# A copy by DMA alone: eight rows per engine walked to and fro

## The chip, the cores and the metric

The kernel runs on one core of one Trainium2 chip. The metric is the time of one execution in microseconds (us), measured on the device. Beside it there is one execution recorded by the hardware profiler; "the profile" and "the trace" are what it left.

## The reference

```python
def setup_inputs():
    return {
        "x": np.random.randn(8192, 8192).astype(np.float32),
    }

def reference(x: np.ndarray) -> np.ndarray:
    return np.fft.ifftshift(x)
```

On an array of even sizes this swaps opposite quadrants: out[i, j] = x[(i + 4096) % 8192, (j + 4096) % 8192]. Nothing is computed; 268.4 MB are read and 268.4 MB are written, all in the chip's main memory (HBM). A row is 8192 x 4 bytes = 32 KB.

## The kernel before, in words

The kernel is a row of DMAs from the input tensor to the output tensor, memory to memory; no tile is kept on the core and no compute engine works. All DMAs are issued by SyncE (SP) through the helper `copy` (lines 25 to 29, where line 26 is the line that the profile shows). It takes a row and a column of the output, adds half of the rows and half of the columns (modulo the size) for the input, and uses the same list of steps and counts (`dims`) on both sides.

The loop (lines 35 to 39) goes down the output in stripes of 128 rows (`rows` = 16 engines x `apart` = 8), 64 stripes in all. In each stripe it issues four DMAs, one for each quarter of the columns (`piece` = 2048 floats, 8 KB): the first quarter (column 0), the third (4096), the second (2048), the fourth (6144). Each DMA is 128 rows of 8 KB, 1 MB; it is spread over 16 DMA engines, so that an engine has eight pieces of 8 KB per DMA. The kernel is written for an engine to have eight neighbouring rows, 32 KB from one to the next and 256 KB from one engine's first row to the next engine's. Each engine goes down its eight rows in one quarter, jumps back to its first row for the next quarter, and after four quarters goes on to the next stripe.

What sets the order: SP issues the 256 DMAs in the order of the program. The framework gives them eight semaphores in turn, so that from the ninth on, a DMA is issued only when the one eight before it has landed. No DMA depends on the data of another.

Of the kernel before, what the change touches and what calls it, by code (L numbers as in the profile page):

```python
# [1 line left out]

# [4 lines left out]


ENGINES = 16  # L10


@with_exitstack
def kernel(
    ctx: ExitStack,
    tc: tile.TileContext,
    x: bass.AP,
    out: bass.AP,
):
    nc = tc.nc  # L20
    R, C = x.shape
    hr = R // 2
    hc = C // 2

    def copy(queue, row, col, dims):
        queue.dma_start(
            out=bass.AP(out.tensor, out.offset + row * C + col, dims),
            in_=bass.AP(x.tensor, x.offset + (row + hr) % R * C + (col + hc) % C, dims),
        )


    apart = 8
    piece = hc // 2
    rows = ENGINES * apart
    for row in range(0, R, rows):
        for col in (0, hc):
            copy(nc.sync, row, col, [[C, rows], [1, piece]])
        for col in (piece, hc + piece):
            copy(nc.sync, row, col, [[C, rows], [1, piece]])


# [1 line left out]
_INS = ['x']  # L43
_OUTS = [((8192, 8192), 'float32')]


def kernel(**inputs):
    import numpy as _np
    import concourse.bacc as _bacc
    import concourse.tile as _tile  # L50
    from concourse import mybir as _mybir
    from concourse.bass_utils import run_bass_kernel_spmd as _run

    nc = _bacc.Bacc("TRN2", target_bir_lowering=False, num_devices=1)  # L54
    arrays, args = {}, []
    for name in _INS:
        a = _np.ascontiguousarray(inputs[name])
        if a.dtype.kind in "iu":
            a = a.astype(_np.int64)
        arrays[f"in_{name}_dram"] = a  # L60
        args.append(nc.dram_tensor(f"in_{name}_dram", a.shape, _mybir.dt.from_np(a.dtype), kind="ExternalInput").ap())
    for i, (shape, dtype) in enumerate(_OUTS):
        dt = _mybir.dt.from_np(_np.dtype(dtype))
        args.append(nc.dram_tensor(f"out_{i}_dram", shape, dt, kind="ExternalOutput").ap())
    with _tile.TileContext(nc) as tc:
        kernel(tc, *args)
    r = _run(nc, [arrays], core_ids=[0])
    got = tuple(r.results[0][f"out_{i}_dram"] for i in range(len(_OUTS)))
    return got[0]
```

## Time and profile before

| what | value |
|---|---|
| median of 3 runs | 814.22 us (814.01, 814.22, 817.59) |
| the profiled execution's own time | 813.0 us |
| its span, first to last instruction | 811.2 us |
| DMAs | 256, of 1 MB each |
| packets of their queue (q1) | 36,864; 98.8% of 16 engines' span |
| median from issue to landing of a DMA | 25.2 us |
| one issue on SP, median | 511 ns |
| read and written together | 662 GB/s over the span |

How to read it: a packet is one contiguous run moved by one DMA engine, here 8 KB of a row, and for each engine and DMA a tiny one that reports the end to a semaphore. The share of a queue is the time that its packets took, summed, by 16 engines' span. The GB/s of the page count each byte once, as it is moved; the memory sees it twice, read and written. "Issue to landing" runs from the instruction on SP to the moment when the last of 16 engines has reported. A line of the windows gives the window, its length, the busy time of GpSimd (which has four small fills at the start and no part in the copy), the clock of TensorE (unused here), the mean busy share of the DMA engines, and GB/s. A line of the waits names who waited, for what, how long in total, how many times, and the longest wait in us.

### The profile page before, as it was taken

What the parts mean: (1) busy time and instruction counts of PE and PEld (TensorE: products, weight loads), DVE (VectorE), ACT (ScalarE), POOL (GpSimd) and SP (SyncE); (2) the same over time, 40 slices, a digit from 0 to 9 for tenths busy, and PEclk for the clock granted to TensorE, in tenths of its full rate; (3) what the DMA queues carried; (4) which work ended last, traced back from release to release, by engine and by line L of the source; (5) the groups of instructions that cost most, each with busy time, mean ns of one, the idle gap of its engine ahead of it and who ended that gap; (6) DMA issues with size and microseconds to landing.
All of it is one profiled execution on the core that took longest, in us unless ns stands there. A gap on an engine that the chain in (4) does not pass through costs nothing. (4 is left out here: it accounts for less than half of the span.)

```text
span 811.2 us, 301 instructions
## 1 busy us (share of the span) xinstructions
POOL 0.2 (0%) x4
## 2 busy tenths in 40 slices
POOL 0000000000000000000000000000000000000000
DMA  8999999999999999999999999999999999999998
GB/s 303 336 329 330 334 336 332 331 333 332 333 333 336 335 335 330 336 331 332 332 332 336 329 336 330 336 327 330 334 336 325 334 334 330 332 330 330 338 330 299
DMA packets 36866, 268.47 MB, mean 331 GB/s; under 512 B 4096, under 2 KB 4096, under 8 KB 4096
## 3 DMA queue, kind: packets, MB, share of 16 engines
q1 hardware_dynamic: 36864, 268.45, 98.8%
q14 instruction: 2, 0.02, 0.0%
HBM read 268.44 MB, written 268.44 MB: 662 GB/s over the span
## 5 line engine op out<-in xcount | busy, mean ns | idle before, releaser
L54 POOL MEMSET const-bfloat16-1.0<- 128x1 bf16 x1 | 0.1, 101 | 0.0
L54 POOL MEMSET const-uint8-127<- 128x1 uint8 x1 | 0.1, 101 | 0.0
L54 POOL MEMSET const-float32-0.0<- 128x1 f32 x1 | 0.1, 98 | 0.2 <-issue 0.2
L54 POOL MEMSET const-float32-1.0<- 128x1 f32 x1 | 0.1, 98 | 0.0
## 6 DMA issues: line engine op xcount, KB each, us to landing
out_dram<-in_x_dram SPq DMA_DIRECT2D x256, 1024.0 KB, 25.2
```

Of the source, the lines that this page charges most:

```text
L54: nc = _bacc.Bacc("TRN2", target_bir_lowering=False, num_devices=1)
```

## The change

The DMAs, their sizes and the order of the quarters stay. The helper now writes a DMA as three steps: 16 engines, each 8 rows (256 KB) from the next; 8 rows per engine; 2048 columns. For the first and second quarter (the first and third DMA of a stripe) the eight rows are taken downward as before; for the third and fourth quarter (the second and fourth DMA) they are taken upward: the start is the engine's last row, and the step from row to row is minus 32 KB, on both the input and the output side. So an engine goes down in the first quarter, up in the third, down in the second, up in the fourth. In the compiled program the downward DMAs are merged again to 128 x 2048, and the upward ones stand as 16 x 8 x 2048. The order of the instructions on SP and the waits are otherwise the same.

```diff
-    def copy(queue, row, col, dims):
+    def copy(queue, row, col, per, size, down):
+
+        first = row if down else row + per - 1
+        dims = [[per * C, ENGINES], [C if down else -C, per], [1, size]]
         queue.dma_start(
-            out=bass.AP(out.tensor, out.offset + row * C + col, dims),
-            in_=bass.AP(x.tensor, x.offset + (row + hr) % R * C + (col + hc) % C, dims),
+            out=bass.AP(out.tensor, out.offset + first * C + col, dims),
+            in_=bass.AP(x.tensor, x.offset + (first + hr) % R * C + (col + hc) % C, dims),
         )
 
 
-    apart = 8
+    per = 8
     piece = hc // 2
-    rows = ENGINES * apart
-    for row in range(0, R, rows):
-        for col in (0, hc):
-            copy(nc.sync, row, col, [[C, rows], [1, piece]])
-        for col in (piece, hc + piece):
-            copy(nc.sync, row, col, [[C, rows], [1, piece]])
+    for row in range(0, R, ENGINES * per):
+        for k, col in enumerate((0, hc, piece, hc + piece)):
+            copy(nc.sync, row, col, per, piece, k % 2 == 0)
```

## The prediction

> **What bounds the kernel now.** I read the page first, then the DMA queue's own waits, then the windows, then the single packets.
>
> The page shows no compute at all; the DMA engines carry the span from the second slice to the last:
>
> ```profile
> span 811.2 us, 301 instructions
> ...
> DMA  8999999999999999999999999999999999999998
> GB/s 303 336 329 330 334 336 332 331 333 332 333 333 336 335 335 330 336 331 332 332 332 336 329 336 330 336 327 330 334 336 325 334 334 330 332 330 330 338 330 299
> DMA packets 36866, 268.47 MB, mean 331 GB/s; under 512 B 4096, under 2 KB 4096, under 8 KB 4096
> ...
> q1 hardware_dynamic: 36864, 268.45, 98.8%
> ...
> HBM read 268.44 MB, written 268.44 MB: 662 GB/s over the span
> ...
> out_dram<-in_x_dram SPq DMA_DIRECT2D x256, 1024.0 KB, 25.2
> ```
>
> See here: 256 DMAs of 1 MB; 36,864 packets, of which 4,096 (16 for each DMA) are tiny and the other 32,768 are the 8 KB pieces of rows; the 16 engines are busy 98.8% of the span; and the rate is flat at about 332 GB/s.
>
> Is it the issuing queue that holds them back? The waits of SP, and the instructions of line 26:
>
> ```profile
> SPq L26 <- DMA out_dram<-in_x_dram: 649.3, 248, 3.3
> ```
> ```profile
> L26 SPq DMA_DIRECT2D out_dram<-in_x_dram x256: 511/511/666, 0.7 to 785.8; - x128
> ```
>
> No. An issue takes 511 ns, 256 of them 131 us; SP waits 649.3 / 248 = 2.62 us ahead of each of the last 248 issues for a DMA that is eight back. The page's 25.2 us to landing is eight DMAs at one per 3.15 us (811.2 less about 4 us of start and end, by 256).
>
> So each DMA engine always has packets; what matters is how long one takes. The windows of the start against the middle:
>
> ```profile
> 2.00:5.00 3.00, 0.00 (x0) 1.00 0.89 328
> 5.00:8.00 3.00, 0.00 (x0) 1.00 1.00 350
> 8.00:11.00 3.00, 0.00 (x0) 1.00 1.01 352
> 11.00:14.00 3.00, 0.00 (x0) 1.00 1.00 341
> 100.00:400.00 300.00, 0.00 (x0) 1.00 0.99 333
> 400.00:700.00 300.00, 0.00 (x0) 1.00 0.99 332
> ```
>
> The last number is GB/s: the same engines with the same share of busy time move 350 to 352 for 6 us, and 332 ever after. The trace's packet records say more. Of the 32,768 packets of 8 KB, 60.0% take 309 ns (309 to 312), the other 40.0% take 511.7 ns on average; the mean is 390.2 ns. Check: 32,768 x 390.2 / 16 = 799.0 us, and 4,096 tiny ones of 9 ns add 2.3 us: 801.3 us, the page's 98.8%. If every packet took 309 ns the data would need 633 us. So an engine's own speed is not the limit: **the memory, read and written at once, stalls four packets in ten.** Only a change in how often it stalls moves the time.
>
> **The change, part by part.** The sum starts from the profiled execution's own 813.0 us: 811.2 of span and 1.8 around it. It lies 1.2 us under the median of the runs, 814.22, and I add those 1.2 at the end.
>
> 1. *What stays.* 256 DMAs, each 16 engines by 8 rows by 8 KB; the same order of quarters (first, third, second, fourth); the same waits on the DMA eight back. The same packets in number and size: 0 us.
>
> 2. *The upward DMAs as instructions.* Compiled, the 128 downward ones are still 128 rows of 2,048; the 128 upward ones become 16 by 8 by 2,048. The trace has no issue of that shape. Below: no cheaper than 511 ns would help, since SP waits anyway. Above: the cover is the 2.62 us wait, and the longest issue in the trace is 666 ns; even at five times 511 ns the wait absorbs it (3.15 us is the interval). If that cover were gone, each upward DMA would delay the next by what it takes over 3.15 us. I take 0.
>
> 3. *The order of the rows in the upward DMAs.* A step from one row to the next is 32 KB back instead of 32 KB forward. The trace has no backward step within a DMA, but each DMA's start is a jump: back by seven rows and sideways (192 times per engine, three in each of the 64 stripes of 128 rows), or on by 121 rows to the next stripe (63 times). If I sort the 8 KB packets by start and cut them into 128s, one cut to a DMA (engines run up to 2 us apart, so the cut is rough), the first 16 packets of a cut average 397 ns after a jump back and 396 ns after a jump to a new stripe. Two very different jumps cost the same, so a sign should cost little: 0, with the bounds of step 4.
>
> 4. *The turns.* At the 192 turns inside stripes, an engine's last row is now its next row too, 16 KB to the side (or, between the third and second quarter, 8 KB), both in x and in out. Before, it moved seven rows away. The trace has no such neighbour step, so I bound it by the two classes of packets. Best: the packet behind a turn is always of the 309 class: (390.2 - 309) x 192 = -15.6 us. Worst: always of the slow class: (511.7 - 390.2) x 192 = +23.3 us. A weaker guide lies between: by the same cuts, the four quarters of a DMA average 404, 392, 380 and 384 ns. The first two rows are 14 ns over the mean of 390, the most that seems to hang on a DMA's beginning: 2 rows x 14 ns x 192 = 5.4 us, which a smoother turn could win and a rougher one pay again. The nearest row is the 397 against 396 above: no dependence on the jump. I take 0.
>
> 5. *Engines close together.* At a turn an engine that leads is back on the row number that a laggard is still on, in another block of eight rows (256 KB apart); before, it was on row 0 while the other was on row 7. Does sharing a row number cost? From the landing records, the spread (standard deviation) of the 16 engines' ends of a DMA grows from 281 ns in the first 32 DMAs to 445 ns between the 193rd and 224th, while the windows stay at 333 and 332 GB/s. Sorted by spread in four equal groups, DMAs follow at 3,151, 3,139, 3,169 and 3,148 ns, with no direction. So 0.
>
> Sum: 813.0 + 0 = 813.0, plus 1.2: **814 us, no change.**
>
> The Trainium skill has a rule that speaks against the change: "DMA: Bandwidth & Descriptors", section "Latency and other measured facts", reports copies whose parallel streams lie a large power of two apart falling from 214 to 164 GB/s at 2 MiB, and to 207 at 512 KiB, and supposes that lock-stepped streams meet on the same channels. Here the engines are 256 KiB apart in both kernels, and the trace's first 2 us, where they are closest in step, have nearly all packets at 309 ns: it does not bear the rule out at this distance. By that rule the turns would push the time towards the slower rival below.
>
> **The rivals.**
>
> *Faster: the memory still has the row at hand.* If an adjacent piece of a row just touched is cheaper, the packets behind 192 turns gain. Place: the first packet of the third, second and fourth quarter. For it: stalls come from the memory, and 350 GB/s in the window from 5 to 11 us proves that it can go faster. Against it: only 3 of 32 packets per engine and stripe are affected, and the 397 and 396 above. Fully it gives 814.2 - 15.6 = 799 us, at half the effect 806. Were the rate of the first windows held throughout (351 instead of 332.5), 268.4 MB would take 765 instead of 807 us: 772 is the floor that I don't expect.
>
> *Slower: the neighbour collides.* The packet behind a turn reads and writes beside what its own predecessor is still doing (in the records a packet starts some 3 ns ahead of the end of the one before), or beside another engine on the same row number. Fully slow: 814.2 + 23.3 = 837.5; at half, 826. It decides from 21 ns per turn on (4.1 us by 192). For it: a packet's cost is two-valued, and the slow class is well populated; with the rows taken backwards, any look-ahead in the memory would be lost on half of the DMAs too. Against it: step 5.
>
> *The change does not do what it says.* The downward DMAs carry no 16 by 8 shape. If their 128 rows are dealt to the engines in another way than eight neighbours each, no engine meets its own row at a turn, and the time stays at 814.
>
> **How the numbers follow.** No change 0.37 (814); faster 0.26; slower 0.31; not doing what it says 0.06 (814). About 0.5%, 4.1 us, is what a measurement of this kernel can tell from no change, so 810 to 818 is "the same". Of the faster case nearly all lies under 810, of the slower one nearly all over 818: faster 0.26, same 0.43, slower 0.31. The range reaches from near the full price of the faster rival to midway between half and full price of the slower: 801 to 832.
>
> **What would show it.** In the page after: still 36,864 packets on q1 and about 98.8%; GB/s between 325 and 338 in each slice. SP: about 2.6 us of wait per issue; an issue of the upward form under 3 us. Packets: the share of 309 ns still near 60%. Steps 3 and 4 are wrong if that share, or the mean of the first 16 packets of a cut (397), moves by over 20 ns against the rest of the DMA; the slower rival shows there as slow packets at the beginning of the cuts, the faster as 309s. Step 5 is wrong if the pace falls where the spread of the landings is small. What would make the whole wrong: a stall share that moves everywhere and not just at the turns, since then the order of the rows sets the pace as a whole.

## The result, and the profile after

The changed kernel takes 812.83 us (median of 22 runs, 811.92 to 813.99), the kernel before 814.37 us (22 runs, 811.77 to 819.77): ratio 0.9977, 95% interval 0.9967 to 0.9988. The forecast was 814, no change, with 810 to 818 counted as the same. The lowest runs are equal, 811.77 and 811.92; the gain lies in the bulk, since the middle half of the runs before is 813.8 to 815.2 and after 812.4 to 813.4.

The page of the changed kernel, the lines that answer to those of before:

```profile
span 810.6 us, 301 instructions
...
GB/s 303 331 334 330 336 334 330 336 333 327 335 335 332 329 332 332 337 334 331 334 331 336 326 331 337 332 334 335 330 332 334 336 332 328 333 333 336 337 330 301
DMA packets 36866, 268.47 MB, mean 331 GB/s; under 512 B 4096, under 2 KB 4096, under 8 KB 4096
...
q1 hardware_dynamic: 36864, 268.45, 99.3%
...
HBM read 268.44 MB, written 268.44 MB: 662 GB/s over the span
...
out_dram<-in_x_dram SPq DMA_DIRECT2D x256, 1024.0 KB, 25.2
```

The same packets at the same 662 GB/s, the same 25.2 us to landing. The span is 0.6 us shorter. Its waits of SP, and the instructions of line 29 (smallest, median, largest duration in ns):

```profile
SPq L29 <- DMA out_dram<-in_x_dram: 633.7, 248, 3.2
```
```profile
L29 SPq DMA_DIRECT2D out_dram<-in_x_dram x256: 537/603/700, 0.7 to 784.7; - x128
```

Issues have become longer: in turn 537 and 603 ns, 572 on average instead of 515. The waits have become shorter by about as much: 633.7 / 248 = 2.56 us instead of 2.62. The cover took it. The windows (last number GB/s):

```profile
2.00:5.00 3.00, 0.00 (x0) 1.00 1.00 330
5.00:8.00 3.00, 0.00 (x0) 1.00 1.00 355
8.00:11.00 3.00, 0.00 (x0) 1.00 1.02 344
11.00:14.00 3.00, 0.00 (x0) 1.00 1.02 339
100.00:400.00 300.00, 0.00 (x0) 1.00 1.00 333
400.00:700.00 300.00, 0.00 (x0) 1.00 1.00 333
```

Again a fast start and then 333 without end. In the packet records 60.2% of the 8 KB packets are of the 309 ns class (60.0% before) and the others average 517.2 ns (511.7). The mean of all is 391.9 ns, where it was 390.2: packets are a little longer in the kernel that is a little faster, and the engines are busy for 99.3 instead of 98.8% of the span.

One thing in these records looked like a mechanism. Cut into 128s as in the prediction, the packets of downward DMAs average 384 ns and those of upward ones 400 ns, and at the turn to the third quarter the first 16 packets average 383 ns, where they had 403 before. (At the turn to the second quarter they rose from 391 to 410, and at the turn to the fourth they went from 397 to 391; the three turns together went from 397 to 395.) So three theories went to the chip: **A**, meeting its own row at a turn saves an engine about 10 ns; **B**, the upward form as such saves; **C**, upward is dear and the turns pay for it; against them the prediction's own, that the order of an engine's rows sets nothing.

### The profile page after: what moved, and what is told of

It reads as the page before. It is cut to its first block, busy times and chain, and to the rows that moved or that the text cites. A ratio compares the mean times of both kernels' runs of the same rounds, so it can differ in the third digit from the quotient of the medians.

```text
span 810.6 us, 301 instructions
## 1 busy us (share of the span) xinstructions
POOL 0.2 (0%) x4
## 3 DMA queue, kind: packets, MB, share of 16 engines
q1 hardware_dynamic: 36864, 268.45, 99.3%
## 6 DMA issues: line engine op xcount, KB each, us to landing
out_dram<-in_x_dram SPq DMA_DIRECT2D x256, 1024.0 KB, 25.2
```

## The experiments

They ran in three sets, each with the kernel before on the same chip: all upward, turning with few meetings, two rows straight and two rows turning on chip 15; the two repeats, two rows with few meetings and the pairs by row on chip 13; the rest on chip 6. On these chips the kernel before takes 823.4 to 823.9 us, 1.1% more than in the result, so only ratios are compared, and ratios of different sets are ratios from different chips.

**All upward, no turn.**

```diff
-        for k, col in enumerate((0, hc, piece, hc + piece)):
-            copy(nc.sync, row, col, per, piece, k % 2 == 0)
+        for col in (0, hc, piece, hc + piece):
+            copy(nc.sync, row, col, per, piece, False)
```

> All 256 DMAs take their eight rows upward (16 x 8 x 2048), so there is no turn: each DMA begins seven rows below the end of the one before. Beside before at 814.4 us and the changed kernel at 812.8 (ratio 0.9977). Theory A, the turns gain: with the turns gone the gain is gone, ratio 1.000 (0.999 to 1.001). Theory B, it is the upward form (direction, or 16 x 8 instead of 128 rows) that gains, wherever the rows lie: twice as many upward DMAs, ratio 0.995. Theory C, two effects cancel: in the trace of the changed kernel the packets of downward DMAs average 384 ns and those of upward ones 400 ns, so upward is dear and the turns pay for it: all upward costs up to (400 - 390) ns x 2,048 packets per engine = 20 us, ratio 1.01 to 1.025.

Measured: 824.21 us, ratio 1.0002 (0.9990 to 1.0014). B and C both fall: 256 upward DMAs of the 16 x 8 x 2048 form cost what 256 downward ones of 128 x 2048 cost. Their issues on SP:

```profile
L29 SPq DMA_DIRECT2D out_dram<-in_x_dram x256: 571/571/690, 0.7 to 796.5; - x128
```

So the 384 against 400 ns of the cut packets was no pace. The landing records (the mean of the 16 engines' ends of a DMA, from the tenth DMA on; a mean here is good to about 10 ns) say so too: in the changed kernel a DMA of the first quarter (down) ends 3,180 ns behind the one ahead of it, of the third (up) 3,099, of the second (down) 3,156 and of the fourth (up) 3,167; before, all down, it was 3,164, 3,126, 3,140 and 3,177. The upward DMAs of the changed kernel come 35 ns sooner than its downward ones, although their packets average 16 ns longer. And in the next kernel, which also goes down and up in turn, the downward packets average 403 ns and the upward ones 389: the sign is turned round.

**Turning with few meetings.** The directions alternate as in the change, but between two stripes. The expectation counts no meeting; one in eight steps is still one, since the fourth quarter of stripe two (up) is followed by the first quarter of the same stripe (down). That makes 32 meetings per engine instead of 192, 24 KB to the side in the output and 8 KB in the input.

```diff
-    for row in range(0, R, ENGINES * per):
-        for k, col in enumerate((0, hc, piece, hc + piece)):
-            copy(nc.sync, row, col, per, piece, k % 2 == 0)
+    stripe = ENGINES * per
+    for row in range(0, R, 2 * stripe):
+        one, two = row, row + stripe
+        for k, col in enumerate((0, hc, piece, hc + piece)):
+            copy(nc.sync, (one, two)[k % 2], col, per, piece, k % 2 == 0)
+        for k, col in enumerate((0, hc, piece, hc + piece)):
+            copy(nc.sync, (two, one)[k % 2], col, per, piece, k % 2 == 0)
```

> Half of the DMAs go downward and half upward, in turn as in the changed kernel, but neighbours in time work on two different stripes of 128 rows, so no engine meets the row that it has just left. Theory A (the turns gain): ratio 1.000, as before. Theory B (the upward form gains): 0.9977, as the changed kernel. Theory C (upward is dear, turns pay): no turn to pay, so slower, up to (400 - 390) ns x 1,024 = 10 us, ratio 1.005 to 1.012. If alternation itself matters because it keeps the engines in step (spread of landings 230 to 312 ns in the changed kernel, 281 to 445 before): 0.9977 with the small spread.

Measured: 822.67 us, 0.9984 (0.9972 to 0.9996), so C falls here too; A is not yet told from "alternation alone". Both kernels then went side by side on chip 13, the changed one and this one:

> The changed kernel once more, on the same chip as the three others of this call. If its gain is real and of its size, the ratio to before is 0.9977 again (0.9967 to 0.9988), whatever the chip's own level. Theory A' (alternating directions gains, the meeting at the turn does nothing): the same ratio as no_meeting_again within 0.001. Theory A (the meeting gains): below it by 0.0015 or more.

> The kernel of no_meeting unchanged, beside the changed kernel itself; the first time it came out at 0.9984 (0.9972 to 0.9996), between the two theories. Alternation alone gains (A'): 0.9977 to 0.9984. The meeting at the turn gains (A): 1.000.

Measured: the changed kernel 822.36 us, 0.9994 (0.9980 to 1.0007); with few meetings 822.85 us, 0.9997 (0.9986 to 1.0007). They differ by 0.0003, far inside either interval: at eight rows 160 meetings more or less do nothing that can be measured, and the 0.0023 of the first comparison comes back as 0.0006, with an interval that holds 1. Nor does alternation keep the engines in step, as one line of the first expectation supposed: the spread of a DMA's 16 ends, by groups of 32 DMAs, is 230 to 311 ns in the first trace of the changed kernel, but 250 to 439 in its trace on chip 13, and was 280 to 445 before.

**More meetings per packet.** One DMA takes two quarters row by row, so that half of all packets follow their neighbour in the same row.

```diff
...
+        def dims(across):
+            return [[per * C, ENGINES], [C, per], [across, 2], [1, size]]
-            out=bass.AP(out.tensor, out.offset + first * C + col, dims),
-            in_=bass.AP(x.tensor, x.offset + (first + hr) % R * C + (col + hc) % C, dims),
+            out=bass.AP(out.tensor, out.offset + row * C + col, dims(hc)),
+            in_=bass.AP(x.tensor, x.offset + (row + hr) % R * C + hc + col, dims(-hc)),
...
-        for k, col in enumerate((0, hc, piece, hc + piece)):
-            copy(nc.sync, row, col, per, piece, k % 2 == 0)
+        for col in (0, piece):
+            copy(nc.sync, row, col, per, piece)
```

> One 2 MB DMA takes two quarters of eight rows per engine, row by row: first the one quarter of a row, then the other quarter of the same row 16 KB to the side, then the next row. So 1,024 of an engine's 2,048 packets follow their neighbour, where the changed kernel has 192 such turns. If meeting one's own row gains 10 ns: ratio 0.987. If it costs 7 ns: 1.009. If it is worth nothing: 0.998 to 1.001 (1,024 steps at nothing; 128 DMAs instead of 256 save 2,048 tiny packets of 9 ns over 16 engines, 1.2 us). At the full prices of the prediction's two classes of packets: 0.90 or 1.15.

Measured: 821.94 us, 0.9988 (0.9976 to 0.9999), that is -1.0 us with about 1.0 us to either side. The expectation puts the 2,048 tiny packets saved at 1.2 us; whether they count at all is doubtful, as the two-row kernels below show. If they don't, 1,024 neighbour steps gain 1 ns each, with 1 ns to either side; if they do, nothing. Theory A is dead at its 10 ns, and so are the full prices of both rivals. The page of this run shows fewer packets, and the mean rate that the changed kernel has on this chip too, 327 GB/s:

```profile
DMA packets 34817, 268.45 MB, mean 327 GB/s; under 512 B 2048, under 2 KB 2048, under 8 KB 2048
```

**More turns per row.** Two rows per engine and DMA (1,024 DMAs of 256 KB): straight, turning, and turning with few meetings (as above, with stripes of 32 rows, so 128 meetings instead of 768). All three have the first edit, the straight kernel the second too.

```diff
-    per = 8
+    per = 2
...
-            copy(nc.sync, row, col, per, piece, k % 2 == 0)
+            copy(nc.sync, row, col, per, piece, True)
```

> Stripes of 32 rows: an engine has two rows of a quarter per DMA, all downward; 1,024 DMAs of 256 KB. It is the control of two_rows_turning. All theories: at or above the time before, since there are four times as many DMAs (12,288 more tiny packets, at 9 ns and 16 engines 7 us, if nothing hides them) and the engines' blocks are 64 KB instead of 256 KB apart; 815 to 835 us. 1,024 issues of 511 ns are 523 us and stay covered.

> As two_rows_straight, but to and fro: 256 stripes with three turns each, 768 turns per engine instead of 192. Theory A (each turn saves (814.4 - 812.5) us / 192 = about 10 ns): 7 to 8 us under two_rows_straight. Theory B (upward form, half of the DMAs as in the changed kernel): 1.5 to 2 us under it. Theory C: of both signs, but a difference of several us. No effect of order at all: equal within 1 us.

> Two rows per engine and DMA, downward and upward in turn as in two_rows_turning, with the same mix of instruction forms, but neighbours in time lie in two different stripes of 32 rows, so no row is met at a turn. two_rows_straight had 0.9988 and two_rows_turning 1.0051. If the meeting at 768 turns is what cost 0.6 per cent there (the prediction's slower rival, 5.1 us / 768 = 7 ns per turn): 0.999. If it is the longer issue of the mixed forms (603 against 510 ns in those traces, at an interval of only 0.8 us per DMA): 1.005. If alternation as such gains, as A' has it: 0.997.

Measured: straight 823.06 us, 0.9988 (0.9975 to 1.0001); **turning 828.17 us, 1.0051 (1.0034 to 1.0068)**, on the same chip; turning with few meetings 822.89 us, 0.9994 (0.9983 to 1.0006), on chip 13. Here is the only case in which to and fro lengthens the time by more than the noise.

The straight kernel says something of the bound as well. It has 12,288 more tiny packets than the kernel before, 7 us by the expectation if nothing hid them, and it takes no longer. Its 8 KB packets average 393.9 ns, where they average 398.9 in the all-upward kernel on the same chip: 5 ns less on 2,048 packets of an engine is 10 us, so the large packets give back what the tiny ones take, as they would if something behind the engines set the pace.

The loss of the turning kernel isn't the longer issue. SP's waits, first the turning kernel, then the one with few meetings:

```profile
SPq L29 <- DMA out_dram<-in_x_dram: 173.8, 479, 1.3
```
```profile
SPq L29 <- DMA out_dram<-in_x_dram: 170.5, 490, 1.2
```

The same cover and the same issues (median 603 ns in both), and 0.0057 apart: 4.7 us, or 7 ns for each of the 640 meetings that the one has more. Against the straight kernel it is 5.1 us, or 7 ns for each of 768. Which meetings? Two kernels keep one kind each: the step between the first and third or second and fourth quarter (512 meetings, 16 KB to the side), and the step from the third to the second quarter (256 meetings, 8 KB to the side in the output and 24 KB in the input, where the expectation has 8 on both sides). The order of stripes one and two, quarters counted from 1, u for up:

```
meet first:   one 1, one 3u, two 1, two 3u, one 2, one 4u, two 2, two 4u
meet second:  one 3u, one 2, two 3u, two 2, one 4u, two 1, one 1, two 4u
```

> Two rows per engine and DMA, downward and upward in turn, with 512 meetings, all of the kind that steps 16 KB to the side (first to third and second to fourth quarter); the step from third to second quarter goes to another stripe. two_rows_turning (768 meetings, of which 256 of the other kind) was at 1.0051, two_rows_no_meeting at 0.9994. Every meeting costs alike (6 ns): 0.9994 + 512 x 6 ns / 823 us = 1.003. Only the other kind costs: 0.9994. Only this kind costs (9 ns each): 1.005. The cost is in having all visits of a row within one stripe's eight packets: 0.9994 too.

> The counterpart: 256 meetings, all of the kind from third to second quarter (8 KB back in the output, 8 KB back in the input too), the other neighbours in different stripes. Every meeting costs 6 ns: 1.001. Only this kind costs (18 ns each): 1.005. Only the 16 KB kind costs, or neither: 0.999 to 1.000.

Measured: 823.49 us, 1.0005 (0.9993 to 1.0017), and 822.89 us, 0.9998 (0.9986 to 1.0010). Over the kernel with few meetings that is 0.0011 and 0.0004, neither outside its interval; together 0.0015, of the 0.0057 that the turning kernel loses. So it is neither kind alone. What it is stays open. Two things are in the turning kernel only: three meetings one after another in the same two rows, and to and fro with all DMAs in turn within one stripe of 32 rows (the other three kernels that go to and fro work on two stripes at once). Neither was tried by itself, and the turning kernel ran on chip 15 alone, the other three on chips 13 and 6.

**The place of the reads.** An engine reads the first of its eight pieces eight times; seven of eight rows of the output are copies of the block's first.

```diff
+        same = [[per * C, ENGINES], [0, per], [1, size]]
-            in_=bass.AP(x.tensor, x.offset + (first + hr) % R * C + (col + hc) % C, dims),
+            in_=bass.AP(x.tensor, x.offset + (first + hr) % R * C + (col + hc) % C, same),
```

> All downward, but an engine reads the first of its eight pieces eight times (source step 0), so the output is not the reference's: seven of eight rows are copies of the block's first. As many bytes are read, but from one eighth of the places, with the same piece read again at once. If the memory's rows being at hand were worth anything to a read, this is its extreme: ratio well under 1 (0.95 or less; at 309 ns for every packet 0.78). If the order and place of the reads do not matter: 0.99 to 1.01. If hitting one place again is dear (a collision): over 1.02.

Measured: 821.05 us, 0.9974 (0.9956 to 0.9991). Reading the same 8 KB again at once, the extreme of "still at hand", is worth 0.26%, where the middle of the faster rival (806 of 814 us) had asked 1% for 192 neighbours in 2,048 packets. The run leaves the writes where they were, so it speaks for the reads alone.

**The distance between the engines.** All downward, the engines' blocks 8 MB apart instead of 256 KB.

```diff
-        dims = [[per * C, ENGINES], [C if down else -C, per], [1, size]]
+        dims = [[hr // ENGINES * C, ENGINES], [C if down else -C, per], [1, size]]
...
-    for row in range(0, R, ENGINES * per):
-        for k, col in enumerate((0, hc, piece, hc + piece)):
-            copy(nc.sync, row, col, per, piece, k % 2 == 0)
+    for half in (0, hr):
+        for row in range(half, half + hr // ENGINES, per):
+            for col in (0, hc, piece, hc + piece):
+                copy(nc.sync, row, col, per, piece, True)
```

> All downward; the engines' blocks of eight rows lie 256 rows, 8 MB, apart instead of 256 KB, so that the engines walk in step at a large power of two. It tests the prediction's step 5 (engines on the same row number of their blocks do not disturb each other) where a disturbance should be strongest. Step 5 right, or the engines too loosely in step: ratio 0.99 to 1.01. If streams this far apart meet in the memory: clearly slower, 1.2 to 2.1 (the Trainium skill's page DMA: Bandwidth & Descriptors, section Latency and other measured facts, has 103 instead of 214 GB/s at 8 MiB; by that alone 2.1).

Measured: 1,468.67 us (four runs, 1,442 to 1,474; no interval was formed), 1.78 times the time before; the fastest of the four is 1.75 times. Its page and its windows:

```profile
q1 hardware_dynamic: 36864, 268.45, 98.3%
...
HBM read 268.44 MB, written 268.44 MB: 366 GB/s over the span
```
```profile
2.00:5.00 3.00, 0.00 (x0) 1.00 0.88 232
5.00:8.00 3.00, 0.00 (x0) 1.00 1.04 202
8.00:11.00 3.00, 0.00 (x0) 1.00 0.94 177
...
100.00:400.00 300.00, 0.00 (x0) 1.00 0.99 183
```

Same packets, same 98% busy, 183 instead of 332 GB/s. 47.5% of the packets are still of the 309 ns class, but the others take 1,061 ns on average instead of 512. Only addresses have changed, the DMA engines look as busy as ever, and no column of busy time tells that the copy takes 1.78 times as long. The edit does two things at once, though: it puts the engines a large power of two apart, and it spreads a DMA over 128 MB on each side instead of 4. Which of the two does it was not tried.

## Why the prediction was right

*The bound.* The memory and not the engines or the queue: borne out. In every kernel the DMA engines are 98 to 100% busy, 12,288 tiny packets more cost nothing, and the time rose by a factor of 1.78 when only the addresses changed. The picture of two classes, and "only a change in how often it stalls moves the time", is not. In the kernel before, from 5 to 11 us, where 351 GB/s are moved, only 9% of the packets are of the 309 ns class, and the mean is 374 ns; from 100 to 400 us 58% are, and the mean is 390 ns at 333 GB/s. The two-row kernel that turns has 64% of them, and of all kernels only the 8 MB one is slower. The others are no class in the kernel before but a spread from 313 ns to over 800, without a second peak. While the engines are always busy, the mean of the packets is the time of the copy, divided by packets: it tells the pace over again, and the share of the 309 ns class doesn't tell even that.

*Step 2, the upward issue.* Taken as 0, hidden under SP's wait: borne out. Issues went to 572 ns on average, and the waits gave up what they took. All upward, at 571 ns, took 1.0002.

*Step 3, the backward steps.* 0: borne out by the all-upward kernel. The reading behind it was close: the 396 ns after a jump to a new stripe includes the kernel's very first packets (609 ns on average), which follow no jump; without them it is 392, against 397 after a jump of seven rows, good to about 8 and 5 ns. The two still agree within that.

*Step 4, the turns.* 0 out of -15.6 to +23.3 us: borne out at eight rows, and in part by luck. No row of the trace had a neighbour step, "the same" had a chance of 0.43, and the 0 was a choice between bounds. The changed kernel and the one with few meetings differ by 0.0003, 0.2 us or under 2 ns for each of 160 meetings, and 1,024 meetings in one kernel came to 0 or 1 ns each. The prediction's sign of being wrong, 20 ns on the first 16 packets of a cut, is nearly met twice, with -20 ns at the turn to the third quarter and +19 at the turn to the second, and the time follows neither. The bounds, a packet always of one class or the other, were far too wide: no order of an engine's own packets that was tried came near either end. That the turn from the third to the second quarter is 8 KB "both in x and in out" is wrong for x, where it is 24 KB (columns 0 and 6144); no term hangs on it. A loss by going to and fro does exist, at two rows: 7 ns a turn, under the 21 ns from which it would have decided here, and not shown to be the prediction's collision. The cut packets' first two rows, "the most that seems to hang on a DMA's beginning", were no prize: the first 16 packets stand 8 ns over the mean after the change (400 against 392), 7 ns before.

*Step 5, engines close together.* 0: right for this change, and its reason reaches less far than it sounds. At 256 KB apart, being on the same row number cost nothing that the eight-row kernels show; with the engines 8 MB apart the copy takes 1.78 times as long. The prediction put the rule of large powers of two aside because the trace's first 2 us "have nearly all packets at 309 ns". They have 55 of 77; and the 8 MB kernel has 39 of 57 in its first 2 us of packets, and 1 of 139 from 5 to 11 us. So that sign couldn't tell the two cases apart, and at 256 KB the prediction was right without evidence from it. The Trainium skill's rule in "DMA: Bandwidth & Descriptors", section "Latency and other measured facts", has 103 of 214 GB/s at 8 MiB, which is 0.48. The run at 8 MB agrees in kind, with 183 of 332, which is 0.55. The distances between 256 KB and 8 MB were not tried, nor one of 8 MB and a little more, and which part of the memory is shared is not shown.

*The third rival.* Whether the 128 rows of a downward DMA are dealt to the engines in eights is not shown by any run. The all-upward kernel, which says so in its steps, has the pace of the kernel before; that fits and does not prove it.

*What stays open.* The 1.5 us of the first comparison. Its interval excludes 1; on chip 13 the same kernel gives 0.9994 with an interval that doesn't, and the kernel with few meetings gives 0.9984 on chip 15 and 0.9997 on chip 13. Kernels without any to and fro come out as low: straight over two rows 0.9988, pairs by row 0.9988, one piece read eight times 0.9974. So a gain of 0.1 to 0.2%, if there is one, can't be put down to alternation, and not to the meeting either.

## What to carry to other kernels

In a copy from memory to memory whose DMA engines are always busy, the order in which one engine takes its own rows (down, up, jumping, meeting a row again) moved the time by 0.6% at most here; where the 16 engines stand relative to each other moved it by a factor of 1.78. Don't take the mean of a group of packets, or the share of fast ones, for a pace: the time between landings is the pace. A sign that is to rule out a rival should be looked for in a kernel that has the rival's fault. A difference of 0.2% on one chip is measured again beside a control that lacks the supposed cause, before it is explained; and the control's steps are counted, since one that seemed to have no meeting had 32.

## What the runs showed that was not expected

The engines' blocks 8 MB apart: 1.78 times the time at an unchanged busy share of 98%. To and fro over two rows: 0.6% more than straight on the same chip, though neither of its two kinds of meeting by itself costs a measurable part. Tiny packets: 12,288 more of them for nothing. And SP's issue has no fixed length: in the kernel of 2 MB DMAs it is the instruction itself that is held, not a wait ahead of it:

```profile
L30 SPq DMA_DIRECT2D out_dram<-in_x_dram x128: 596/5972/14510, 0.7 to 777.1; - x128
```

Its median is 5,972 ns, near the interval of 6.37 us between landings of those DMAs, with no wait for a DMA among its 128 issues, and the shortest takes 596 ns. It reads as an instruction held up until there is room for it, and not as a dear one; what is full then is not shown.
